# Two small tiles take the slots of others in the memory map of a one-core decoder trunk

## The chip, the core and the metric

The kernel runs on one core of a Trainium2 chip. The metric is the device time of one execution in microseconds; several runs are made and the median is given. The profile is of one execution. TensorE is named PE in it (PEld is its loading of stationary operands), VectorE DVE, ScalarE ACT, GpSimd POOL, and SyncE SP, which only issues DMAs here.

## What is computed

Two decoder layers over 1024 tokens of width 1024, in float32. Layer 0 mixes tokens with HGRN2, a gated linear recurrence with 8 heads of 128; layer 1 with attention in a sliding window of 128 tokens (16 query heads, 4 shared key/value heads, a sink per head, a relative bias). Each layer ends with a gated FFN with a causal convolution of width 3, of inner width 2816, and each sub-layer with a LayerNorm of the scaled residual. Cut to its frame:

```python
h = x
for layer in range(2):
    if layer < 1:
        mix = hgrn2_mixer(h, hgrn_w_in[layer], lower_bounds[layer], hgrn_gnorm_w[layer], hgrn_w_out[layer])
    else:
        mix = swa_sink_mixer(h, k_shared, v_shared, swa_w_q[0], swa_sinks[0], bias, mask, swa_w_out[0])
    h = layer_norm(ALPHA * h + mix, ln_mix_g[layer], ln_mix_b[layer])
    ff = conv_ffn(h, ffn_w_in[layer], ffn_conv_w[layer], ffn_conv_b[layer], ffn_w_out[layer])
    h = layer_norm(ALPHA * h + ff, ln_ffn_g[layer], ln_ffn_b[layer])
    if layer == 0:
        k_flat, v_flat = jnp.split(h @ shared_w_kv, 2, axis=-1)
```

## The kernel before

**Split products.** A float32 operand is kept as two tiles of a rounded format (fp32r), a high part and the low rest. `mm3` (L193 to L197) makes one step of a product from three matmuls: high on high (L194), the high stationary part with the low moving part (L195), and the low stationary part with the high moving part (L196). In each, 128 stationary columns (512 bytes in a partition) are loaded, and 512 moving columns (2048 bytes) run past them. `mm32` (L200) makes a plain float32 matmul, `tr` (L204) a transpose.

**Stages.** First comes HGRN2 (to about 590 us). Its first head's weights are split into the tiles qp, tot, St and og. The weights of the other seven heads pass through a ring WR of 8 rows; for each of these heads two units of work (q with the forget gate, values with the output gate) take 7 half-size block products each by Winograd's scheme, in place of 8. The moving operands are x, transposed, in T, and block sums of it in HL. Between these products lie the recurrence's small matmuls, which wait for VectorE and ScalarE. Then the output projection and layer 0's FFN follow: a first product over 22 blocks of columns, again 7 products of 12 matmuls each (`Up.product`, `Up.collect`, `Up.run`), with the weights in HL and HT as stationary and T and TX as moving operands; then a second product (`Down`) with operands in a ring over HL, T and HT. Attention follows (about 1230 to 1500 us), then layer 1's FFN. In `Up.run` the order of products in a block is 1, 2, 6, 7, 4, 5, 3; products 1, 2, 4 and 5 have T as moving operand, 3, 6 and 7 have TX.

**Order.** TensorE's order is written by hand throughout, that of ScalarE and VectorE in HGRN2 and attention too, with a running estimate of time (`Order`) that says when a piece of a chain is laid.

**Memory map.** Pools lie one behind another in every partition, and a tile that is asked for again under the same name takes a slot of its earlier ones (`bufs` slots, in turn). The pool cp holds T and HL. Behind it, at byte 118,784, the pool sm holds small tiles with two slots each: warm (a one-column tile that ScalarE writes to have a table loaded), ss, st, mv, rs, tick, nm, dn; a slot takes 32 bytes or a multiple. Behind sm and a tile of 128 bytes begin in turn, at one address, the tiles of HGRN2 and the tile Y, with the FFN's and the attention's behind Y. The tiles of HGRN2's pool hp end with cr (two slots of 512 bytes, for the convolution's parameters), rb (the table of relative bias, 64 bytes) and oh; WR lies behind them. The starts that matter, in bytes of a partition:

| tile | used as | start before | past a multiple of 512 |
|---|---|---|---|
| T | moving, stationary | 4,096 | 0 |
| HL | moving, stationary | 69,632 | 0 |
| Y (and raw, VG, ...) | not in 512-column products | 119,872 | 64 |
| HT | stationary | 152,640 | 64 |
| qp, tot, St, og | stationary (first head) | 162,368 to 174,656 | 64 |
| TX | moving | 177,216 | 64 |
| WR | stationary | 195,712 | 128 |

Every row within these tiles is a multiple of 512 bytes long, and every operand of a 512-column product begins a multiple of 512 bytes from its tile's start.

**The two tiles.** In `Up.run`, behind products 2 and 4 of a block, GpSimd copies one column of Y into tick (L539, L540) and issues a DMA behind that copy; the copy serves as a marker in GpSimd's order, and nothing reads tick. In `conv_params` ScalarE's queue loads cr four times, TensorE transposes each (L1000), then rb is allocated (L1005), loaded by ScalarE's queue (L1006) and used by one matmul (L1011).

Of the kernel before, what the change touches and what calls it, by code (L numbers as in the profile page):

```python
# [10 lines left out]
F32 = mybir.dt.float32  # L11
# [5 lines left out]
P = 128  # L17
# [90 lines left out]
def trunk(ctx: ExitStack, tc: tile.TileContext, a: dict, out: bass.AP):  # L108
# [6 lines left out]
    sm = ctx.enter_context(tc.tile_pool(name="sm", bufs=2))  # L115
# [24 lines left out]
    def psmm():  # L140
        return mmp.tile([P, 512], F32, name="psmm")

    def psax():
        return axp.tile([P, 1024], F32, name="psax")
# [229 lines left out]
    class Up:  # L374
# [131 lines left out]
        def run(self, ready, down):  # L506

            od.finish(ready[:4])
            tiles = [psax(), psax()]
            ax = [tiles[i % 2][:, i // 2 * 512:(i // 2 + 1) * 512] for i in range(4)]  # L510

            for (p, fc), ps in zip([(p, fc) for p in (4, 5) for fc in range(2)], ax):
                self.product(p, fc, ps)
            od.finish(ready[4:])
            mm = [psmm() for _ in range(4)]
            self.pairs = [mm, ax]
            for (p, fc), ps in zip([(p, fc) for p in (1, 2) for fc in range(2)], mm):
                self.collect(p, fc, self.product(p, fc, ps))
            for fc in range(2):
                self.collect(6, fc, self.product(6, fc, mm[fc]))  # L520
            for fc in range(2):
                self.collect(7, fc, self.product(7, fc, mm[2 + fc]))
                self.collect(4, fc, ax[fc])
                self.collect(5, fc, ax[2 + fc])
            self.weights(2)
            sums = down.sum_blocks()
            for fc in range(2):
                self.collect(3, fc, self.product(3, fc, mm[fc]))
            banks, n = mm[2:] + ax[:2] + mm[:2] + ax[2:], 0
            for fc in range(2, NF):  # L530
                if fc > 2:
                    self.weights(fc)
                for p in (1, 2, 6, 7, 4, 5, 3):
                    self.collect(p, fc, self.product(p, fc, banks[n % 8]))
                    n += 1
                    if p in (2, 4):
                        transfer = next(sums, None)
                        if transfer:
                            tick = sm.tile([P, 1], F32, name="tick")  # L539
                            with tc.issue_after(nc.gpsimd.tensor_copy(tick, Y[:, 2 * (fc % 2) + (p == 4), :1]).ins):  # L540
                                transfer()
                    if fc == NF - 1 and p in (1, 6, 4):
                        down.ahead.append(down.operands(0, len(down.ahead)))
# [156 lines left out]
    with tc.tile_pool(name="t", bufs=1, reuse_waits="tile") as raws, hgrn_pool as hp:  # L700
# [170 lines left out]
        with tc.tile_pool(name="ep", bufs=1, reuse_waits="tile") as ep:  # L871
# [29 lines left out]
            warm = sm.tile([P, 1], F32, name="warm")  # L901
# [85 lines left out]
        def conv_params():  # L987
            yield 330.0
            for l in range(2):
                crs = []  # L990
                for k in range(2):
                    crs.append(hp.tile([88, P], F32, name="cr", bufs=2))
                    for j in range(2):
                        q = 2 * k + j
                        src = a["ffn_conv_w"][l, q] if q < 3 else a["ffn_conv_b"][l]
                        nc.scalar.dma_start(crs[k][44 * j:44 * (j + 1), :], src.rearrange("(c p) -> c p", p=P))
                yield 10.0
                for k, cr in enumerate(crs):
                    ps = psax()
                    nc.tensor.transpose(ps[:, :88], cr, ident[:88, :88])  # L1000
                    nc.vector.tensor_copy(cwt[:, l, 2 * k:2 * k + 2, :],
                                          ps[:, :88].rearrange("p (a b) -> p a b", a=2))
                    yield 3.0

            rb = hp.tile([32, 16], F32, name="rb")  # L1005
            nc.scalar.dma_start(rb, a["rel_bias"])  # L1006
            oh = hp.tile([32, 2 * P], F32, name="oh")
            nc.scalar.dma_start(oh, a["onehot"])
            yield 10.0
            ps = psax()  # L1010
            nc.tensor.matmul(ps[:16, :2 * P], rb, oh, start=True, stop=True)  # L1011
            rl = hp.tile([16, 2 * P], F32, name="oh")
            nc.vector.tensor_scalar(rl, ps[:16, :2 * P], -1.0, None, op0=ALU.mult)
            yield 3.0
            nc.scalar.dma_start(rbd, rl)

        params = od.spawn(conv_params())

        def recur(h, qs, fg, kp):
# [935 lines left out]
```

## Time and profile before

| | us |
|---|---|
| median of 3 runs | 2198.88 (2198.08 to 2199.84) |
| the profiled execution | 2198.49 |
| its span, first to last instruction | 2196.6 |
| PE busy | 2124.2 |
| DVE busy | 1801.9 |
| ACT busy | 971.9 |
| POOL busy | 251.1 |

The mean granted clock of TensorE is 0.986. A matmul's printed time runs until its modelled end and overlaps the next one's, so the pace of a stream of matmuls is read from the distance between starts (the timeline) or from the count in a window, not from the mean time of one.

### The profile page before, as it was taken

The page shows a single profiled execution, that of the slowest core. Times are in us where ns is not written, and L with a number is a line of the kernel's source. Part 1 is how long each engine was busy: PE and PEld are TensorE (multiplying, and loading weights), DVE is VectorE, ACT ScalarE, POOL GpSimd, SP SyncE. Part 2 cuts the span into 40 slices and gives each one's busy share as a digit, 9 for nine tenths or more (in the row PEclk, how much of TensorE's full clock was granted, in tenths as well). Part 3 has the DMA queues.
Part 4 walks back from the last instruction along what each step waited for, and adds up shares of the span by engine and source line. Part 5 has one row for each costly group of instructions (what it writes and reads, how often), then busy time and mean ns, then how long its engine had stood idle before and what let it go on. Part 6 is the DMA issues. An engine that isn't in the chain of part 4 may idle for free.

```text
span 2196.6 us, 31745 instructions
## 1 busy us (share of the span) xinstructions
PE 2124.2 (97%) x12303; PEld 1753.6 (80%) x12303; DVE 1801.9 (82%) x2445; ACT 971.9 (44%) x1556; POOL 251.1 (11%) x278
## 2 busy tenths in 40 slices
PE   9789999988899999999999999999999999999998
PEld 7568777777688888888888888888888888888887
DVE  6667777665899999887897758978999998878986
ACT  6445554452344444443442246752444444444430
POOL 1000000000103112110000103231021121100001
PEclk9899999999999999999999999999999999999999
DMA  4011211131434548754975431133245587549762
GB/s 157 20 47 34 66 36 43 51 99 69 142 96 143 176 161 168 154 132 141 320 232 180 155 87 37 44 100 112 90 136 182 159 166 156 138 134 311 240 203 105
DMA packets 241487, 286.82 MB, mean 131 GB/s; under 512 B 30088, under 2 KB 160312, under 8 KB 241336
## 3 DMA queue, kind: packets, MB, share of 16 engines
q1 hardware_dynamic: 222464, 238.26, 34.0%
q0 software_dynamic: 18016, 46.16, 10.0%
q8 instruction: 97, 1.59, 0.3%
q14 instruction: 54, 0.44, 0.1%
q10 hardware_dynamic: 856, 0.37, 0.1%
HBM read 241.72 MB, written 89.15 MB: 151 GB/s over the span
## 4 chain that ended last, share of the span: by engine, by line
PE 87%; DVE 7%; ACT 3%; issue 1%; DMA 1%; SPq 0%; DVEq 0%; ACTq 0%
PE psmm L194 17%; PE psmm L196 17%; PE psmm L195 17%; PE psax L194 9%; PE psax L196 9%; PE psax L195 9%; PE psax L200 3%; PE psmm L204 1%; PE psmm L200 1%; PE psax L1729 1%; PE psax L204 1%; DVE qp L1089 1%; PE psmm L1563 1%; DVE kp L1091 1%; DVE WR L169 1%
## 5 line engine op out<-in xcount | busy, mean ns | idle before, releaser
L498 DVE SCALAR_TENSOR_TENSOR Y<-Y,cwt 128x1023 f32<-128x1023 f32 (+1 forms) x176 | 224.9, 1281 | 49.0 <-ACT Y L496 47.0
L221 ACT CAST HL<-rx 128x1024 fp32r<-128x1024 f32 (+1 forms) x151 | 150.4, 1003 | 167.2 <-DMA rx<-in_ffn_w_in_dram 29.9
L194 PE MATMUL psmm<-T,HL 128*128 128x512 f32 x512 | 201.4, 393 | 0.0
L196 PE MATMUL psmm<-T,HL 128*128 128x512 f32 x512 | 199.7, 390 | 0.0
L195 PE MATMUL psmm<-T,HL 128*128 128x512 f32 x512 | 199.4, 389 | 0.0
L169 DVE TENSOR_TENSOR HL<-rx,HL 128x1024 fp32r<-128x1024 f32 (+1 forms) x151 | 178.4, 1187 | 18.4 <-ACT HL L221 18.3
L496 ACT ACTIVATE Y<-Y,cwt 128x1024 f32<-128x1024 f32 x88 | 108.7, 1238 | 95.1 <-DVE Y L485 90.1
L194 PE MATMUL psax<-T,HL 128*128 128x512 f32 x352 | 138.0, 392 | 0.0
L196 PE MATMUL psax<-T,HL 128*128 128x512 f32 x352 | 137.4, 390 | 0.0
L195 PE MATMUL psax<-T,HL 128*128 128x512 f32 x352 | 137.1, 390 | 0.0
L243 POOL TENSOR_TENSOR rs<-rs,nhalf 128x1 f32<-128x1 f32 x32 | 44.1, 1377 | 742.8 <-DVE rs L242 742.8
L196 PEld LDWEIGHTS psmm<-T,HL 128*128 128x128 f32 x512 | 96.1, 188 | 20.8
L195 PEld LDWEIGHTS psmm<-T,HL 128*128 128x128 f32 x512 | 96.2, 188 | 19.9
L194 PEld LDWEIGHTS psmm<-T,HL 128*128 128x128 f32 x512 | 96.1, 188 | 19.9 <-ACT Vt L1664 0.2
L540 POOL COPY tick<-Y 128x1 f32<-128x1 f32 x64 | 61.8, 966 | 358.0 <-DVE Y L479 354.4
L194 PE MATMUL psmm<-HL,WR 128*128 128x512 f32 x168 | 73.5, 437 | 29.2 <-ACT fg L1309 8.2
L221 ACT CAST HT<-rx 128x1024 fp32r<-128x1024 f32 (+1 forms) x37 | 35.5, 960 | 131.4 <-DVE rx L452 78.7
L194 PE MATMUL psmm<-T,WR 128*128 128x512 f32 x224 | 91.0, 406 | 2.7 <-ACT WR L1241 2.7
L196 PE MATMUL psmm<-T,WR 128*128 128x512 f32 x224 | 88.9, 397 | 0.0
L195 PE MATMUL psmm<-T,WR 128*128 128x512 f32 x224 | 88.8, 396 | 0.0
L169 DVE TENSOR_TENSOR WR<-raw,WR 128x512 fp32r<-128x512 f32 x84 | 63.0, 775 | 30.0 <-ACT WR L1241 29.2
L221 ACT CAST HL<-Y 128x1024 fp32r<-128x1024 f32 (+1 forms) x32 | 28.5, 890 | 114.4 <-DVE Y L452 49.2
(407 smaller groups left out, 5993.9 us busy)
## 6 DMA issues: line engine op xcount, KB each, us to landing
rx<-in_ffn_w_in_dram SPq DMA_DIRECT2D x136, 256.0 KB
rx<-gd SPq DMA_DIRECT2D x118, 256.0 KB
bsd<-in_ffn_w_out_dram POOLq DMA_DIRECT2D x36, 768.0 KB, 6.7
gd<-Y SPq DMA_DIRECT2D x44, 512.0 KB
raw<-in_hgrn_w_in_dram SPq DMA_DIRECT2D x30, 512.0 KB
rx<-in_ffn_w_out_dram SPq DMA_DIRECT2D x54, 256.0 KB
R<-bsd SPq DMA_DIRECT2D x44, 256.0 KB
Y<-in_ffn_w_in_dram SPq DMA_DIRECT2D x40, 256.0 KB
```

The lines of the kernel that those rows point to most:

```text
L169: make = lambda e: e.tensor_tensor(lo, src, hi.bitcast(F32), op=ALU.subtract)
L194: nc.tensor.matmul(ps, st(0), mv(0), start=start, stop=False, skip_group_check=more)
L195: nc.tensor.matmul(ps, st(0), mv(1), start=False, stop=False, skip_group_check=more)
L196: nc.tensor.matmul(ps, st(1), mv(0), start=False, stop=stop, skip_group_check=more)
L200: nc.tensor.matmul(ps, lhsT, rhs, start=start, stop=stop, **kw)
L204: nc.tensor.transpose(ps, src, ident)
L221: nc.scalar.copy(hi, src)
L243: nc.gpsimd.tensor_tensor(rs, rs, nhalf, op=ALU.pow)
L496: nc.scalar.activation(c, u, AF.Identity, bias=cwt[:, l, 3, ci:ci + 1], scale=cwt[:, l, 2, ci:ci + 1])
L498: nc.vector.scalar_tensor_tensor(c[:, sh:], u[:, :S - sh], cwt[:, l, 2 - sh, ci:ci + 1], c[:, sh:], op0=ALU.mult, op1=ALU.add)
L540: with tc.issue_after(nc.gpsimd.tensor_copy(tick, Y[:, 2 * (fc % 2) + (p == 4), :1]).ins):
L1089: nc.vector.tensor_tensor(qv[:, :, 1, :], qv[:, :, 1, :], tv[:, :, 0:1].to_broadcast([P, nb, m]), op=ALU.mult)
```

## The change

The tile tick is now allocated under the name warm, and rb as a corner of a tile under the name cr. Neither has slots of its own any more: the pool sm is 64 bytes shorter, and hp another 64.

```diff
@@ -536,7 +536,7 @@
                     if p in (2, 4):
                         transfer = next(sums, None)
                         if transfer:
-                            tick = sm.tile([P, 1], F32, name="tick")
+                            tick = sm.tile([P, 1], F32, name="warm")
                             with tc.issue_after(nc.gpsimd.tensor_copy(tick, Y[:, 2 * (fc % 2) + (p == 4), :1]).ins):
                                 transfer()
                     if fc == NF - 1 and p in (1, 6, 4):
@@ -1002,7 +1002,7 @@
                                           ps[:, :88].rearrange("p (a b) -> p a b", a=2))
                     yield 3.0
 
-            rb = hp.tile([32, 16], F32, name="rb")
+            rb = hp.tile([88, P], F32, name="cr", bufs=2)[:32, :16]
             nc.scalar.dma_start(rb, a["rel_bias"])
             oh = hp.tile([32, 2 * P], F32, name="oh")
             nc.scalar.dma_start(oh, a["onehot"])
```

Y and all that shared its start or lies behind it now begin 64 bytes lower (Y at 119,808, HT at 152,576, TX at 177,152), and oh, WR and the tiles behind them 128 bytes lower (WR at 195,584). T, HL and the tiles of cp stay. With that HT, TX, qp, tot, St, og and WR begin at multiples of 512.

The instructions of every engine stand in the order of before. On ScalarE, late in HGRN2 (at 477 us in the profile), the load of rb (and of oh, the one-hot buckets) stands as before, with the name of its target changed and with the wait that it had:

```order
 L1076 COPY fg<-qp 128x128x4 [waits DVE_49]
 L1077 COPY fg<-kp 128x128x4 [waits DVE_49]
-L1006 DMA rb<-in_rel_bias_dram 32x16 [waits DMAHW6_49]
+L1006 DMA cr<-in_rel_bias_dram 32x16 [waits DMAHW6_49]
 L1008 DMA oh<-in_onehot_dram 32x256 [waits DMAHW7_49]
 L1461 CAST HL<-raw_101 128x1024
```

Nothing moved there but the name. On TensorE the matmul that uses it (kd holds keys, psax and psmm are in PSUM) stands among the last products of HGRN2:

```order
 L195 MATMUL psmm<-HL,WR 128x512
 L196 MATMUL psmm<-HL,WR 128x512
-L1011 MATMUL psax<-oh,rb 16x256
+L1011 MATMUL psax<-oh,cr 16x256
 L1563 MATMUL psmm<-HL,T 128x512 x19
 L200 MATMUL psax<-kd 32x16 x32
```

Its place is the same too. VectorE's and SyncE's orders are the same word for word, and on GpSimd only the name of the 64 copies' target differs.

## The prediction

> **What bounds the kernel now.** I read the page first: busy time, the forty slices, the chain that ended last.
>
> ```profile
> PE 2124.2 (97%) x12303; PEld 1753.6 (80%) x12303; DVE 1801.9 (82%) x2445; ACT 971.9 (44%) x1556; POOL 251.1 (11%) x278
> PE   9789999988899999999999999999999999999998
> PEclk9899999999999999999999999999999999999999
> PE 87%; DVE 7%; ACT 3%; issue 1%; DMA 1%; SPq 0%; DVEq 0%; ACTq 0%
> ```
>
> TensorE is busy for 97% of the span and is 87% of the chain. But for the last slice, those below 9 lie in the first eleven (each 54.9 us), so the other 13% of the chain lies almost wholly in HGRN2, before 590 us. Then windows of the two long product stages, and for the FFN start, where VectorE is fullest (columns: busy us and instructions of PE, PEld, DVE, ACT, POOL; clock; DMA share; GB/s).
>
> ```profile
> 600.00:700.00 100.00, 100.00 (x460) 82.78 (x459) 95.57 (x123) 46.72 (x61) 17.74 (x14) 1.00 0.37 120
> 640.00:1040.00 400.00, 400.00 (x1751) 328.49 (x1750) 360.58 (x399) 173.05 (x191) 62.82 (x66) 1.00 0.57 151
> 2000.00:2180.00 180.00, 180.00 (x793) 148.61 (x792) 155.22 (x197) 64.43 (x63) 8.38 (x6) 1.00 0.64 214
> ```
>
> TensorE never waits here, at full clock. So what counts is the step from one matmul's start to the next. It is not the same in the two: 400/1751 = 228.4 ns in the FFN's first product (640 to 1040), 180/793 = 227.0 ns in its second. Only starts in order of time show why, since the printed 0.39 us of each matmul overlaps its neighbours. First the second product, where moving and stationary operand both lie in T:
>
> ```profile
> 1103.13 0.39 PE L194 MATMUL psmm<-T 128*128 128x512 f32 x1
> ...
> 1107.89 0.39 PE L194 MATMUL psmm<-T 128*128 128x512 f32 x1
> ```
>
> 21 steps (these two rows and the 20 between them) in 4.76 us: **226.7 ns**. That is the floor that this trace shows for 512 columns; twelve matmuls, one product, take 2.72 us. Now eight products of the first stage in a row, each by its first matmul:
>
> ```profile
> 957.27 0.40 PE L194 MATMUL psmm<-T,HL 128*128 128x512 f32 x1
> ...
> 960.04 0.39 PE L194 MATMUL psax<-T,HL 128*128 128x512 f32 x1
> ...
> 962.76 0.40 PE L194 MATMUL psax<-TX,HL 128*128 128x512 f32 x1
> ...
> 965.52 0.40 PE L194 MATMUL psmm<-T,HL 128*128 128x512 f32 x1
> ...
> 968.29 0.39 PE L194 MATMUL psmm<-T,HL 128*128 128x512 f32 x1
> ...
> 971.01 0.39 PE L194 MATMUL psax<-TX,HT 128*128 128x512 f32 x1
> ...
> 973.78 0.39 PE L194 MATMUL psax<-TX,HT 128*128 128x512 f32 x1
> ...
> 976.50 0.39 PE L194 MATMUL psmm<-T,HL 128*128 128x512 f32 x1
> ```
>
> The products take 2.77, 2.72, 2.76, 2.77, 2.72, 2.77 and 2.72 us. By the memory map, T and HL begin at a multiple of 512 bytes, TX and HT at 64 bytes past one. TX on HL, offsets unlike, takes 2.76. T on HL takes 2.77 right behind a TX product and 2.72 in the product after it; TX on HT, alike again, takes 2.77 first and 2.72 next. So unlike offsets cost, alike ones do not, and each change of offset costs one product some 0.05 us until the stream is back in step. A wait on another engine does not explain it: the view of waits lists none for PE after 600 us. In HGRN2 the stationary weights are the unlike ones, WR at 128 past a multiple, the first head's St and og at 64:
>
> ```profile
> 57.71 0.39 PE L194 MATMUL psmm<-T,St 128*128 128x512 f32 x1
> ...
> 60.04 0.39 PE L195 MATMUL psmm<-T,St 128*128 128x512 f32 x1
> 186.28 0.40 PE L194 MATMUL psmm<-T,WR 128*128 128x512 f32 x1
> ...
> 197.44 0.40 PE L194 MATMUL psmm<-T,WR 128*128 128x512 f32 x1
> ```
>
> Ten steps in 2.33 us are 233 ns; 48 steps in 11.16 us are 232.5 ns. Offset 64 and offset 128, in the same high part of the memory and against the same T, step differently, which points to the offset and not to the place.
>
> **The change part by part.** It removes no instruction, adds none, moves none; it slides Y and all pools behind it down by 64 bytes, and WR by 128. Afterwards T, HL, TX, HT and WR all lie at multiples of 512.
>
> *FFN, first product.* 22 column blocks per layer, each 84 matmuls. Two starts, 16 blocks apart:
>
> ```profile
> 715.79 0.40 PE L194 MATMUL psmm<-T,HL 128*128 128x512 f32 x1
> ...
> 1023.11 0.40 PE L194 MATMUL psmm<-T,HL 128*128 128x512 f32 x1
> ```
>
> 307.32/16 = 19.21 us per block; at the floor 84 x 226.7 ns = 19.04. 0.165 us x 44 blocks = **7.2 us**, all on the chain.
>
> *FFN second product, projections, attention.* Operands lie mostly in T and HL, with a change of offset only where the ring of weights passes HT. The row 2000 to 2180 has 180 - 793 x 0.2267 = 0.25 us above the floor. Adding all steps of 512 columns after 600 us, less the 7.2, I get 2.2 us; some of that is the stream entering from shorter matmuls. Bounds 0.3 and 2.2; I take **2.0**.
>
> *HGRN2.* 7 products of 12 matmuls for 14 units of heads 1 to 7 are 1176, at 5.8 ns above the floor: 6.8 us. The first head's 96, at 6.3 ns: 0.6. Together 7.4, but only what is on the chain counts:
>
> ```profile
> by line: PE psmm L194 11.8%; PE psax L200 11.8%; PE psmm L196 11.0%; PE psmm L195 10.8%; issue 3.7%; PE psax L204 3.5%; DVE qp L1089 2.5%; PE psmm L1563 2.1%; DVE kp L1091 2.0%; DVE WR L169 2.0%; DVE raw L1248 1.8%; DVE Ab L1032 1.7%; DVE T
> ```
>
> ```profile
> 60.00:490.00 430.00, 299.84 (x1176) 0.95 0.17 51
> ```
>
> The first row is the chain from 0 to 590 us: the three lines of the split product (L194 to L196) hold 11.8 + 11.0 + 10.8 = 33.6%, 198 us. The second is WR's matmuls, 300 us busy; with the first head's 96 and the first of the FFN some 330 us lie in that stretch, so 60% of them are on the chain. Where they are not, TensorE only comes sooner to a wait for VectorE or ScalarE. 0.6 x 7.4 = **4.4 us**; the ends are 0 (every gain waited away) and 7.4.
>
> *What else the new addresses touch.* VectorE and ScalarE read and write the same tiles. Three rows, TX from rx (offsets alike), T from rx and T from R (unlike):
>
> ```profile
> L169 DVE TENSOR_TENSOR TX<-rx,TX 128x1024 fp32r<-128x1024 f32 x12 | 14.3, 1219 | 9.3 <-ACT TX L221 9.3
> L169 DVE TENSOR_TENSOR T<-rx,T 128x1024 fp32r<-128x1024 f32 x34 | 40.8, 1218 | 8.0 <-ACT T L221 7.7
> L169 DVE TENSOR_TENSOR T<-R,T 128x1024 fp32r<-128x1024 f32 x30 | 36.2, 1218 | 0.2
> ```
>
> 1219, 1218 and 1218 ns: VectorE is not touched by it, and I take nothing for it, nor for ScalarE's copies. Products of 256 columns: HL on T has both at a multiple of 512, the scores' Kh and q both at 64 past one.
>
> ```profile
> L194 PE MATMUL psmm<-HL,T 128*128 128x256 f32 x64 | 18.2, 284 | 0.0
> L1729 PE MATMUL psax<-Kh,q 128*128 128x256 f32 x112 | 16.3, 285 | 0.0
> ```
>
> 284 and 285 ns: nothing to win or lose. For the small fp32 matmuls of HGRN2, whose operands shift together, no row stands beside another offset; between -1 and +1 us, taken as nothing.
>
> *The two tiles.* "tick" takes the slots of "warm", "rb" one of "cr", which the transposes of the conv parameters must have read first:
>
> ```profile
> L540 POOL COPY tick<-Y x64: 509/1045/2183, 670.3 to 1891.8; 128x1 f32<-128x1 f32 x64
> L1844 ACT ACTIVATE warm<-nhalf x1: 204/204/204, 1310.1 to 1310.1; 128x1 f32<-128x1 f32 x1
> ```
>
> GpSimd's 32 ticks of layer 0 fall into its first FFN product, which is over by 1050 us, those of layer 1 come after 1570: ScalarE's write to warm at 1310.1 is hundreds of us from both, and nobody reads either tile.
>
> ```profile
> 474.63 0.29 PE L1000 MATMUL psax<-ident,cr 88*128 88x88 f32 x1 [2.12 <-DVE og L1198]
> ...
> 476.73 0.33 ACTq L1006 DMA_DIRECT2D rb<-in_rel_bias_dram  x1
> ```
>
> The last of these transposes ends at 474.9, the load is issued at 476.7, 1.8 us later; ScalarE's order shows no new wait before it. Nothing. If that cover were gone, the casts of the output weights (L1461) behind it on ScalarE would wait for those 1.8 us at most.
>
> **Sum.** 7.2 + 2.0 + 4.4 = 13.6 us. The profiled execution took 2198.49 us (span 2196.6 and 1.9 around it), 0.4 below the median of 2198.88. 2198.5 - 13.6 = **2185 us**.
>
> What could eat it in the FFN: VectorE, 95.6% busy from 600 to 700. A TensorE faster by 0.8% asks 96.4% of it; and in its first product 360.58/400 = 90% becomes 91%. It stays off the bound.
>
> **The rivals.**
>
> *A: nothing changes.* The extra steps could hang on the place (tiles beyond HL, in the upper part) and not on the offset: T and HL lie low, TX, HT and WR high, and low on low and high on high run at the floor just as alike on alike do. The change moves no tile across. For it: in this trace place and offset go nearly together. Against: St and WR, both high and both against T, give 233 and 232.5 ns. It would give 2199. A rule of the Trainium skill stands on this side: "TensorE: Matmul & The Clock Gate", Part 2, step 1, says that TensorE has two independent SBUF read ports and that loading the next weights takes no read bandwidth from the running matmul. By it no address would matter and the sum would be 0; the trace, with 2.72 and 2.77 us for one kind of product, does not agree, or the loss lies elsewhere than in that port. Chance 0.11.
>
> *B: slower, the aligned pair itself is what is dear.* At 957.27 and 965.52 T on HL, both at multiples of 512, takes 2.77 us. If that were the cost of certain aligned pairs rather than what is left of a change of offset, TX and HT, once aligned, would join them. All seven products at 2.77: 19.39 against 19.21 us per block, 0.18 x 44 = +7.9 us; WR's products (11.16/4 = 2.79) would win 0.02 x 98 x 0.6 = 1.2: 2205 us. It decides from a mean product of 2.744 us upward. Against it: T on T stays at 2.72, and 960.04 and 968.29 are aligned and at the floor. Chance 0.07.
>
> *C: HGRN2 gives nothing.* TensorE waits there for ScalarE and VectorE, and its clock is granted at 0.95 on the mean; a shifted wait can move a stretch of half clock in or out, some 2 us either way. The FFN's 9.2 us alone give 2189, with such a loss 2191 to 2193. Chance 0.20.
>
> **How the numbers follow.** Forecast (2180 to 2188) 0.62, C 0.20, A 0.11, B 0.07. Faster by over 0.2% (4.4 us, about what a measurement of this kernel can tell from no change): 0.62 + 0.20 = 0.82; same 0.11; slower 0.07. The range takes in forecast and C: below, 7.2 + 2.2 + 7.4 + 2 of clock = 18.8, so 2180, one less for the small matmuls; above 2193. A and B stay out with 0.18: **2179 to 2193**.
>
> **What would show it.** Right: from 640 to 1040 us some 1765 matmuls instead of 1751 (226.7 ns), each product 2.72 us whatever lies ahead of it, the WR stream at 226.7 ns too, no new PE wait after 600. A would show the old 2.72 and 2.77 in the same order; B 2.77 nearly everywhere. C would show the WR stream at the floor, but PE's idle time before 590 us, ahead of L194 <- ACT fg and DVE fg, longer by as much. The prediction is wrong in its main step if the first FFN product keeps its 19.2 us per block.

## The result, and the profile after

The changed kernel takes 2183.39 us (median of 4 runs, 2181.40 to 2187.04), against 2198.48 of the kernel before measured beside it: a ratio of 0.9935, 95% interval 0.9917 to 0.9953, 15.1 us less. The profiled execution took 2187.04, with a span of 2185.1, and is the slowest of the four; it ends 11.5 us ahead of before's. The page after, its busy times and chain:

```profile
PE 2112.8 (97%) x12303; PEld 1756.2 (80%) x12303; DVE 1801.2 (82%) x2445; ACT 971.0 (44%) x1556; POOL 253.1 (12%) x278
PE 88%; DVE 7%; ACT 3%; issue 1%; DMA 1%; SPq 0%; DVEq 0%; ACTq 0%
```

TensorE is 11.4 us shorter busy; VectorE's time has changed by 0.7 us, ScalarE's by 0.9. The windows of the changed kernel that answer to those of before (the FFN's first and second product of one layer each; columns as above, the second moved ahead as it ends earlier):

```profile
600.00:700.00 100.00, 100.00 (x464) 83.25 (x463) 96.34 (x121) 48.26 (x63) 17.73 (x14) 1.00 0.37 119
640.00:1040.00 400.00, 400.00 (x1767) 331.38 (x1766) 365.89 (x403) 175.66 (x194) 64.27 (x66) 1.00 0.57 152
1990.00:2160.00 170.00, 170.00 (x752) 140.90 (x751) 146.57 (x186) 63.44 (x62) 5.76 (x4) 1.00 0.65 219
```

1767 matmuls instead of 1751 pass in 400 us, 226.4 ns each within the count's rounding; the second product is at 170/752 = 226.1. VectorE has gone from 95.6 to 96.3% at the FFN's start, and no wait of TensorE stands after 600 us, as before. The timeline of the changed kernel, first matmuls of products, shows that the pace no longer depends on what lies ahead:

```profile
949.07 0.39 PE L194 MATMUL psmm<-TX,HL 128*128 128x512 f32 x1
...
951.79 0.39 PE L194 MATMUL psmm<-T,HL 128*128 128x512 f32 x1
...
954.51 0.39 PE L194 MATMUL psax<-T,HL 128*128 128x512 f32 x1
...
957.23 0.39 PE L194 MATMUL psax<-TX,HL 128*128 128x512 f32 x1
...
959.95 0.39 PE L194 MATMUL psmm<-T,HL 128*128 128x512 f32 x1
...
962.67 0.39 PE L194 MATMUL psmm<-T,HL 128*128 128x512 f32 x1
...
965.39 0.39 PE L194 MATMUL psax<-TX,HT 128*128 128x512 f32 x1
```

Every product takes 2.72 us. In HGRN2, in the changed kernel's timeline again:

```profile
58.16 0.39 PE L194 MATMUL psmm<-T,St 128*128 128x512 f32 x1
...
60.43 0.39 PE L195 MATMUL psmm<-T,St 128*128 128x512 f32 x1
184.89 0.39 PE L194 MATMUL psmm<-T,WR 128*128 128x512 f32 x1
...
195.77 0.39 PE L194 MATMUL psmm<-T,WR 128*128 128x512 f32 x1
```

Ten steps in 2.27 us and 48 in 10.88 us: 227 and 226.7 ns, where there were 233 and 232.5.

The mean over all steps of WR below 245 ns (longer ones stand at half clock or behind a wait) is less good than these 48: 228.2 ns with T as moving operand and 228.7 with HL, where the kernel before had 232.5 and 232.3.

The first product's stretch of layer 0, from its first to its last matmul with TX, in the kernel before:

```profile
641.80 0.39 PE L194 MATMUL psmm<-TX,HT 128*128 128x512 f32 x1
...
1042.14 0.39 PE L196 MATMUL psax<-TX,HT 128*128 128x512 f32 x1
```

and in the changed kernel:

```profile
638.99 0.39 PE L194 MATMUL psmm<-TX,HT 128*128 128x512 f32 x1
...
1035.88 0.39 PE L196 MATMUL psax<-TX,HT 128*128 128x512 f32 x1
```

It is 3.45 us shorter. TX is in use earlier than that: the second half of each output projection has TX as moving operand and T as stationary one, so the first matmul with TX (at 555.17 us before) belongs to the projection. Where the time went, cut at such matmuls in the two traces:

| stretch | before, us | after, us | difference |
|---|---|---|---|
| start to the first matmul with TX (HGRN2, first half of the projection) | 555.17 | 552.45 | -2.7 |
| on to the first with TX on HL or HT, layer 0 (second half of the projection, LayerNorm, start of the first product) | 86.63 | 86.54 | -0.1 |
| on to the last with TX, layer 0 (first product) | 400.34 | 396.89 | -3.45 |
| on to the first score (second product, K, V) | 265.23 | 264.29 | -0.9 |
| on to the first matmul with TX of layer 1 (attention, first half of the projection) | 197.86 | 198.16 | +0.3 |
| on to the first with TX on HL or HT, layer 1 | 72.81 | 72.42 | -0.4 |
| on to the last with TX, layer 1 (first product) | 400.33 | 396.89 | -3.4 |
| on to the end | 218.22 | 217.50 | -0.7 |

### The profile page after: what moved, and what is told of

It reads as the page before. It is cut to its first block, busy times and chain, and to the rows that moved or that the text cites. A ratio compares the mean times of both kernels' runs of the same rounds, so it can differ in the third digit from the quotient of the medians.

```text
span 2185.1 us, 31745 instructions
## 1 busy us (share of the span) xinstructions
PE 2112.8 (97%) x12303; PEld 1756.2 (80%) x12303; DVE 1801.2 (82%) x2445; ACT 971.0 (44%) x1556; POOL 253.1 (12%) x278
## 4 chain that ended last, share of the span: by engine, by line
PE 88%; DVE 7%; ACT 3%; issue 1%; DMA 1%; SPq 0%; DVEq 0%; ACTq 0%
PE psmm L194 17%; PE psmm L196 17%; PE psmm L195 17%; PE psax L194 9%; PE psax L195 9%; PE psax L196 9%; PE psax L200 3%; PE psmm L204 1%; PE psmm L200 1%; PE psax L1729 1%; PE psax L204 1%; DVE qp L1089 1%; PE psmm L1563 1%; DVE kp L1091 1%; DVE WR L169 1%
## 5 line engine op out<-in xcount | busy, mean ns | idle before, releaser
L540 POOL COPY warm<-Y 128x1 f32<-128x1 f32 x64 | 65.0, 1015 | 353.7 <-DVE Y L479 350.1
```

## The experiments

Two theories stood at the start. **R**: what counts is how far the moving operand's start lies from the stationary one's, modulo some number of bytes. **M**: each operand has to begin at a multiple of 512 itself. The rivals A (place, not offset) and B (aligned pairs are dear) of the prediction stand beside them. All edits are to the changed kernel, and "T on St" means T moving past stationary columns of St; "edge" and "rim" are unused tiles, at the end of the pool cp ahead of T, and behind the pool sm ahead of Y and all that follows.

### All operands alike, none at a multiple

This kernel is called all64.

```diff
-    edge = cp.tile([P, 120], F32, name="edge")
+    edge = cp.tile([P, 136], F32, name="edge")
```

> The changed kernel with T, HL and everything behind them moved up by 64 bytes, so that all operands of the 512-column products lie alike at 64 past a multiple of 512, none at a multiple. Theory R (only the difference between the moving and the stationary operand's offset counts): floor everywhere, about 1765 matmuls from 640 to 1040 us, WR stream at 226.7 ns, time as the changed kernel, 2181 to 2187. Theory M (each operand has to begin at a multiple of 512): all products off the floor, 229 to 233 ns, fewer than 1750 matmuls in that window, 2197 or more.

Measured: 2185.21 us, ratio 0.9943 (0.9929 to 0.9956). The window of this kernel:

```profile
640.00:1040.00 400.00, 400.00 (x1766) 331.21 (x1765) 365.99 (x404) 175.97 (x195) 62.55 (x66) 1.00 0.57 153
```

1766, against 1767 in the changed kernel. The first head's products, T on St and on og, step at 226.7 ns. So M falls: being at a multiple of 512 is not needed, it is enough that all operands lie alike. A falls with it and with the change itself: no tile was moved from low to high, and the steps of low on high came to the floor.

### Each of the two edits alone

tick_only:

```diff
-            rb = hp.tile([88, P], F32, name="cr", bufs=2)[:32, :16]
+            rb = hp.tile([32, 16], F32, name="rb")
```

> Only tick takes the slots of warm; rb keeps its own slot. Y, HT, TX and the first head's qp, tot, St, og lie at multiples of 512, WR at 64 past one. Both theories: the FFN at the floor (1765 matmuls from 640 to 1040), WR's stream at about 233 ns as St's was. By the prediction's terms 7.2 + 2.0 and 0.6 x 0.6 of 13.6 are kept: 2189. If HGRN2's gain was on the chain by more than 60%, the time is higher (2191 at 100%); if by none, it equals the changed kernel's 2183 to 2185.

rb_only:

```diff
-                            tick = sm.tile([P, 1], F32, name="warm")
+                            tick = sm.tile([P, 1], F32, name="tick")
```

> Only rb takes a slot of cr; tick keeps its own. Y, HT, TX, qp, tot, St, og and now WR lie at 64 past a multiple of 512, T and HL at multiples. Theory R: the FFN as before (1751 matmuls from 640 to 1040), WR at about 233 ns instead of 232.5: 2198, no change. Theory M: the same. A rival, that WR alone carries the gain, would give 2186.

Measured on one chip: tick_only 2188.49 us, 0.9953 (0.9940 to 0.9965); rb_only 2196.58, 0.9998 (0.9989 to 1.0007). The window of tick_only, then that of rb_only:

```profile
640.00:1040.00 400.00, 400.00 (x1767) 331.20 (x1766) 364.22 (x401) 174.09 (x192) 63.10 (x66) 1.00 0.57 152
```

```profile
640.00:1040.00 400.00, 400.00 (x1751) 328.42 (x1751) 363.27 (x400) 173.14 (x191) 62.86 (x66) 1.00 0.56 150
```

With tick alone the FFN is at the floor and WR, now at 64, at 233.3 ns, and the time is the expected one (2189). With rb alone nothing is at the floor, since WR only came from 128 to 64. By the medians on this chip tick alone brings 9.1 us, and rb without tick nothing that can be told from the scatter. all64, measured on the same chip with WR and all else alike, is another 3.3 us faster than tick_only.

### How far apart: 256, 128 and 32 bytes

The three kernels widen rim, for 256 bytes so (64 and 40 in place of 96 for 128 and 32 bytes):

```diff
-    rim = sp.tile([P, 32], F32, name="rim")
+    rim = sp.tile([P, 96], F32, name="rim")
```

> The changed kernel with everything behind HL moved up by 256 bytes: Y, HT, TX, St, WR at 256 past a multiple of 512, T and HL at multiples. If the steps depend on the offset modulo 512 (or more), products with TX on HL, TX on HT first, T on WR leave the floor: fewer than 1760 matmuls from 640 to 1040. If only the offset modulo 128 or 256 counts, it is as the changed kernel, 1765, WR at 226.7 ns.

> The changed kernel with everything behind HL moved up by 128 bytes: TX, HT, St, WR at 128 past a multiple of 256, T and HL at 0. If the offset modulo 256 counts: T on WR at 232.5 ns as WR at 128 had it in the kernel before, T on St the same, TX on HL off the floor (228 to 233 ns), TX on HT back to 226.7 after the first product; 1740 to 1755 matmuls from 640 to 1040. If only the offset modulo 128 counts: floor, 1766.

> The changed kernel with everything behind HL moved up by 32 bytes: TX, HT, St, WR at 32 past a multiple of 256. If the lost time goes with the distance (St at 64: 6.7 ns, 16 of its 4-byte columns), T on St takes about 230 ns. If only steps of 64 bytes count, 226.7 and 1766 matmuls from 640 to 1040; if any unlike offset costs the same, 233.

One run each: 2184.99, 2199.32 and 2202.39 us. Runs of one kernel lie up to 6 us apart, so what counts here is the steps and not these times. The windows of up256, up128 and up32 in turn:

```profile
640.00:1040.00 400.00, 400.00 (x1766) 331.22 (x1765) 365.71 (x402) 176.13 (x194) 62.55 (x66) 1.00 0.58 154
```

```profile
640.00:1040.00 400.00, 400.00 (x1751) 328.54 (x1750) 360.72 (x398) 172.59 (x190) 61.67 (x66) 1.00 0.57 151
```

```profile
640.00:1040.00 400.00, 400.00 (x1744) 327.09 (x1743) 359.85 (x397) 171.89 (x189) 61.96 (x66) 1.00 0.57 150
```

A distance of 256 is as good as none; 128 and 32 are not. The steps, as means of start to next start over all such matmuls of a trace (steps over 245 ns left out). With T on St and og it is the stationary operand that starts further on, with TX on HL the moving one:

| distance in bytes | T on St and og, ns | TX on HL, ns | matmuls, 640 to 1040 us | trace |
|---|---|---|---|---|
| 0 | 226.7 | 226.7 | 1767 | after |
| 32 | 233.4 | 233.5 | 1744 | up32 |
| 64 | 233.3 | 229.8 | 1751 | before |
| 128 | 232.2 | 232.8 | 1751 | up128 |
| 256 | 226.7 | 226.7 | 1766 | up256 |

The loss is not in proportion to the distance: with T on St, 32 bytes cost as much as 64. At 64 bytes it goes with the direction. Where the stationary operand is the one further on, T on WR and HL on WR have 233.3 and 233.4 ns as well (tick_only); where it is the moving one, TX on T has 229.2 (before) and TX on HT 229.7 (the kernel tx64 below). Of the three cases set out for up32 the third came nearest, the full loss for any unlike offset; it leaves out the direction. The timeline of up32 shows it:

```profile
57.79 0.40 PE L194 MATMUL psmm<-T,St 128*128 128x512 f32 x1
...
60.13 0.40 PE L195 MATMUL psmm<-T,St 128*128 128x512 f32 x1
```

Ten steps in 2.34 us are 234 ns. At 128 bytes T on WR has 232.5 ns, as it had before, where WR lay at 128 already: the case of the offset modulo 256.

### One tile off

```diff
+            self.gap = pool.tile([P, 16], F32, name="gap")
             self.TX = pool.tile([P, 3, 2, 4, 512], F32R, name="TX")
```

> The changed kernel with 64 unused bytes ahead of TX alone: TX at 64 past a multiple of 256, T, HL, HT, WR, St, og at 0. If the offset of one operand against the other is all that counts, TX on HL and now TX on HT too step at 229.6 ns or more and T on HL behind them loses its start: some 1750 matmuls from 640 to 1040 us, while T on WR stays at 228.2 and T on St at 226.7. The time is the changed kernel's with the FFN's 7.2 us given back, 2190 to 2192. A rival, that the change helps by something other than these steps, would leave it at 2184.

Measured: 2193.99 us, 0.9988 (0.9979 to 0.9997). Window and products of tx64:

```profile
640.00:1040.00 400.00, 400.00 (x1747) 327.60 (x1746) 362.15 (x398) 174.69 (x192) 61.90 (x66) 1.00 0.57 152
```

```profile
956.47 0.40 PE L194 MATMUL psax<-TX,HL 128*128 128x512 f32 x1
...
959.24 0.40 PE L194 MATMUL psmm<-T,HL 128*128 128x512 f32 x1
...
962.01 0.39 PE L194 MATMUL psmm<-T,HL 128*128 128x512 f32 x1
```

TX on HL takes 2.77 us and T on HL behind it, both at multiples of 512 and untouched by the edit, 2.77 as well. So that product's loss is left over from its neighbour, and not a cost of the aligned pair: B falls. The time lies 10.4 us over the changed kernel's on that chip; the expected 2190 to 2192 would have been 6.4 to 8.4. The expectation gave back only the 7.2 us of the kernel before, but here the products of TX on HT, which were alike in that kernel, are off too (229.7 ns): the stretch of the first product is 4.4 us longer in each layer than in the changed kernel (401.33 against 396.89).

### The transposes' operand

In the kernel ident0, ident, the moving operand of the transposes, comes from 128 past a multiple of 256 to a multiple (the small tiles between it and edge move with it); T stays:

```diff
+    lead = cp.tile([P, 32], F32, name="lead")
     ident = cp.tile([P, P], F32, name="ident")
...
-    edge = cp.tile([P, 120], F32, name="edge")
+    edge = cp.tile([P, 88], F32, name="edge")
```

> The changed kernel with ident (the moving operand of every transpose) moved from 128 past a multiple of 256 bytes to a multiple, T and all behind it as they were. If a change of offset costs the next product some 0.02 to 0.05 us wherever it comes from, the T on HL products behind transposes in attention lose that: the steps above the floor from 1300 to 1450 us fall from 0.5 us to under 0.2, those of HGRN2 from 2.0 to about 1, the time by 1 to 2 us, to about 2182. If transposes do not disturb the stream, nothing changes: 2183.4.

Measured: 2183.39 us, 0.9939 (0.9927 to 0.9952), beside 2183.87 of the changed kernel on that chip: no difference. What the steps of 512 columns have above the floor from 1300 to 1500 us adds up to 0.63 us, much as after (0.66; before 0.38). The first products behind transposes in attention still start off the floor; ident's offset is not why, and what is was left open.

### What WR is worth, and how far the runs scatter

The changed kernel was run twice more, once as the measure for ident0 and once beside tick_only, repeated:

> The changed kernel once more, as the measure for the next ones and for how far its runs scatter: 2181 to 2187, 0.9935 of before. Its HGRN2 part (to the first TX matmul) ended at 552.5 us in its first profile and at 555.2 in that of before; by the forecast's 4.4 us it should on the mean end near 551.

> Only tick takes the slots of warm: WR at 64 past a multiple of 256, all else at 0, beside the changed kernel on one chip. WR's 1176 matmuls are 5 to 6.7 ns slower each, 6 to 8 us busy. If 60% of them are on the chain as forecast, it takes 4.0 us more than the changed kernel; 6.8 if all are, 0 if VectorE and ScalarE take it all up in waits.

> The changed kernel, as the measure for the other two on the same chip: 2181 to 2187.

Measured: the changed kernel 2183.87 us, 0.9938 (0.9924 to 0.9951), and 2183.59, 0.9943 (0.9931 to 0.9956); tick_only 2187.04, 0.9954 (0.9942 to 0.9967). On one chip WR's offset is worth 2187.04 - 2183.59 = 3.5 us, where 4.0 were expected, with intervals that overlap; all64 beside tick_only gave 3.3. WR's matmuls are busy for

```profile
60.00:490.00 430.00, 300.72 (x1176) 0.96 0.16 51
```

in tick_only, repeated, and for

```profile
60.00:490.00 430.00, 294.33 (x1176) 0.96 0.16 51
```

in the changed kernel's third trace: 6.4 us less busy, time at half clock included, of which 3.5 by the medians reached the end, about a half.

## Why the prediction was right

**The mechanism.** The forecast put the whole gain into the step from start to start, 226.7 ns where offsets are alike and 229 to 233 where not, with part of a product lost at each change of offset. The changed kernel's timeline, tick_only, all64 and tx64 show each of these. A sentence of the Trainium skill stood against it in the prediction, in "TensorE: Matmul & The Clock Gate", Part 2, step 1: the moving operand and the loading of weights have read ports of their own. Taken as a rule on time, that addresses do not matter, it does not hold here, where up to 7 ns in 227 hang on where the two operands begin. The page itself says nothing of addresses, and no run shows in which part of the reading the time is lost.

**FFN, first product, 7.2 us.** Measured: 3.45 in each layer, 6.9 together.

**Second product, projections, attention, 2.0 us.** By the two traces 2.1 us won and 0.3 lost in attention, 1.8 in all. The forecast's words name only HT as unlike here. The second half of each output projection, TX on T, is unlike too (229.2 ns a step before, 227.4 after); its sum over all steps held most of that. The loss had no term: from 1300 to 1500 us the steps above the floor rose from 0.38 to 0.66 us, and why was left open. That the scores themselves have nothing to win or lose was read from printed times of 284 and 285 ns, which overlap; by their starts Kh on q steps at 118.2 ns before and 118.8 after, less than 0.1 us in all.

**These two together, 9.2 us.** From the first matmul with TX to the end, the changed kernel's three traces and tick_only's two take 1631.7 to 1632.7 us, before and rb_only 1641.4 and 1641.2: 9.2 us on the mean, as forecast.

**HGRN2, 4.4 us.** The forecast took 60% of 7.4. Two of its sizes were off, in opposite directions. WR's stream was to come to 226.7 ns throughout, 5.8 ns a step; on the mean a step won about 4 (232.5 to 228.2 with T, 232.3 to 228.7 with HL), so WR's 1176 are worth some 4.7 us and not 6.8, and what holds the others off the floor was not tested. And more than 60% of it reached the end, as follows. That the term came out near 4.4 is in part luck.

The one profile after shows 2.7, but one profile is not enough here: the first TX matmul starts at 552.5, 550.2 and 549.3 us in the changed kernel's three traces, and at 551.0 in rb_only's, whose WR steps are no faster than before's. The view of the tile TX (count, least, median and greatest ns, first and last start) of the changed kernel's third trace, then of rb_only:

```profile
L194 PE MATMUL psmm<-TX,T x128: 387/389/774, 549.3 to 1542.4; 128*128 128x512 f32 x128
```

```profile
L194 PE MATMUL psmm<-TX,T x128: 388/394/776, 551.0 to 1549.4; 128*128 128x512 f32 x128
```

The rows of WR's matmuls from 60 to 490 us, of rb_only and of tick_only (its first trace):

```profile
60.00:490.00 430.00, 299.91 (x1176) 0.97 0.17 51
```

```profile
60.00:490.00 430.00, 301.29 (x1176) 0.95 0.16 51
```

Both have WR at 64 and the same 233.3 ns at full clock; the clock granted was 0.97 in one and 0.95 in the other, and HGRN2 ended 4.1 us apart (551.0 and 555.1). All traces together tell more. Start of the first matmul with TX, with the clock granted from 0 to 550 us:

| WR | traces | start, us | mean |
|---|---|---|---|
| unlike | before, tick_only, up128 (clock 0.95) | 555.2, 555.1, 555.3 | |
| unlike | tick_only repeated, up32 (0.96) | 554.5, 555.2 | |
| unlike | rb_only (0.97) | 551.0 | 554.4 (all six) |
| alike | the changed kernel's three, all64, up256, tx64, ident0 (0.96) | 552.5, 550.2, 549.3, 551.0, 550.5, 549.0, 551.8 | 550.6 |

The lines of tick_only repeated and of up32, for the two traces with WR unlike at a clock of 0.96:

```profile
L194 PE MATMUL psmm<-TX,T x128: 387/389/776, 554.5 to 1548.1; 128*128 128x512 f32 x128
```

```profile
L194 PE MATMUL psmm<-TX,T x128: 392/396/776, 555.2 to 1556.3; 128*128 128x512 f32 x128
```

With WR alike the stretch ends 3.8 us earlier on the mean, and at a clock of 0.96 every one of the seven ends ahead of these two. rb_only, with the highest clock, is the exception. 3.8 us of the 5.3 that WR and the first head together lost in steps (4.7 and 0.6) is about 70%, from traces that scatter by some 3 us.

**The sum.** 13.6 forecast; 15.1, 14.4 and 13.6 us in the three comparisons of medians with the changed kernel, and 9.2 + 3.8 = 13.0 by the parts.

**The two tiles.** No cost of the shared slots shows, as forecast: rb_only, with rb in cr's slot, is 0.9998 of before, and tick_only keeps the FFN at the floor with the ticks in warm's slots.

**The rivals.** A is out by the change itself and by all64, B by tx64. C, that HGRN2 gives nothing, does not fit the thirteen traces, nor the medians of 2183.4 to 2183.9 where it had 2189; the two pairs on one chip (3.5 and 3.3 us) would each leave it open alone.

## What to carry to other kernels

Where a stream of matmuls has no waits and still a pace that differs from product to product, take the distances between starts, and compare the operands' start addresses. Here the operands had to start alike modulo 256 bytes, at a multiple of 512 or all at 64 past one, and 64 bytes of a small tile in front of the pools cost some 9 of 2198 us. It is not enough that each product's two operands match: a stream that passes from one residue to another loses time at the passage too. A gain in a stage that waits for other engines is worth its share of the chain, and a stage whose clock changes from run to run needs several traces before its term is read.

## What the runs showed of the hardware that was not expected

At a distance of 64 bytes the direction counts: 233.3 ns a step where the stationary operand starts further on (T on St), 229.8 where the moving one does (TX on HL). At 32 bytes both have 233.4 to 233.5, at 256 both are at the floor, 226.7.

Passing from one offset to another costs the product behind it up to 0.05 us, although its own operands are alike; what the forecast did not tell is that the loss depends on the passage. In the kernel before, from 663 to 1042 us, T on HL takes 2.77 us behind TX on HL. TX on HT takes 2.76 behind T on HL, where both products have distance zero and only the offset changes, from 0 to 64; T on HL takes 2.73 in the other direction. The floor, 2.72, is back after three to ten matmuls.
